# The last pair of down tiles of two feed-forwards: eight of 22 inner tiles by seven block products

## The chip, the cores and the metric

The kernel runs on one core of a Trainium2 chip. The metric is the device time of one execution in microseconds (us). Three runs of the kernel before took 1550.16, 1548.57 and 1549.10 us; the median is 1549.1. Engines are called as in the profile: PE is TensorE, whose weight loads (PEld) run beside its matmuls; DVE is VectorE, ACT is ScalarE, POOL is GpSimd, SP is SyncE, which here only issues transfers.

## What is computed

One inference step of one encoder layer, for 512 new frames of one stream and 64 frames of another. The two are put together as 576 token columns; the model is 1024 wide and the feed-forward 2816. All of it is fp32.

```python
h = LN1(alpha*x + 0.5*FFN1(x))
z = h @ w_in            # mLSTM q,k,v,o,i,f | attention q,k,v | branch gates
h = LN2(alpha*h + w_out(sig(g_m)*P_m(mLSTM(h)) + sig(g_a)*P_a(BandAttn(h))))
y = LN3(alpha*h + 0.5*FFN2(h))

def swiglu_ffn(x, w_gu, w_down):
    gate, up = jnp.split(x @ w_gu, 2, axis=-1)
    return (jax.nn.silu(gate) * up) @ w_down
```

The change touches only `@ w_down`, the down projection, in both feed-forwards. Its product has 1024 output rows (8 tiles of 128, called down tiles here, 0 to 7), 2816 inner rows (22 inner tiles of 128) and 576 columns.

## The kernel before

**Numbers.** Every fp32 operand is split into a high part, rounded to fp32r, and a low part, the rest; one product of two tiles is three matmuls: high x high, high x low, low x high (`mm`, line 133). The high part of a weight is made on ACT (`act`, line 147), the low part by a subtraction on DVE (`tt`, line 150). Activations stand in SBUF as such pairs; weights are split as they arrive.

**Order of the work.** PE follows the order in which the program issues its matmuls. The other engines are ordered at compile time by priority; some steps have a raised priority (`HOT`). A small clock in the program (`Order`) adds up an estimate for each matmul, and `later(dt, fn)` issues a step once that clock has gone on by `dt`; `od.force` issues steps early when their result is needed.

**Weights.** `plan` is the list of all weight chunks in the order of use. `pump` issues for each a load into a `wr` tile (two buffers, on SP's queue, line 266) and its split into `wh` and `wl` (four buffers each). `take` gives a chunk to a product, `done` frees it.

**A feed-forward** (`ffn`) makes 22 inner tiles and then the down tiles, in this order: tiles 0 and 1 together (`joined`); the pairs (2, 3) and (4, 5) by `down_pair`, with `DS = (2, 4)`; tiles 6 and 7 (`LAST[n]` = 6) by plain products. An inner dimension of 22 is cut in three chunks, `DC = ((0, 8), (8, 8), (16, 6))`, as first inner tile and number.

**The block products.** In a pair, inner tiles 8 to 15 don't go by plain products but by a scheme of Strassen's kind. The 2 x 8 weight tiles are seen as 2 x 2 blocks of four tiles, the activations as 2 x 2 blocks of four inner tiles by 288 columns (`HT_` = 576 / 2). `seven` then does seven block products instead of eight. Each is four inner tiles x 3 matmuls of 288 columns, into three PSUM banks X, Y and Z. The combined activations (`Inner`) are made once and used by both pairs. The combined weights are made by `split_ds` from two raw chunks, in four steps: "a" (split of the first), "u" (two sums and their split), "t" (two more sums and their split) and "b" (split of half of the second). After each product `step` says what is to be added where: `Norm.take` adds or subtracts a bank to the running tile `d[j]` or `d[j + 1]` of the layer norm on DVE, at `HOT` priority.

**Tiles 6 and 7 before.** `gemm` passes over token halves: tile 6 and tile 7 for the first half of the columns, then both for the second. `HALVES` is 256 and 320 columns in feed-forward 1, and 320 and 256 in feed-forward 2. Each pass goes over all three chunks, so every chunk of the two tiles is loaded and split twice.

**The layer norm behind it** (`Norm`). `collect` adds the bank of one tile and half to `d[j]` and adds to the running sums `s1`, `s2` (`moments`). When tile 7 of a half is in, `stats` makes mean and variance with small matmuls, `rsqrt` the factor (POOL), `centre` subtracts (tiles 6 and 7 on POOL, the rest on DVE), `spread` brings the factor to all partitions by a matmul, and `apply` scales each tile j. In feed-forward 1 `apply` also makes the high and low parts for the next stage, whose first products (`gemm` with `WAVE_M`, four weight chunks) start with the first half. In feed-forward 2 the first half is scaled and stored to `y` in the same way; the second half is turned to token rows by transposes, scaled and stored (`turned`, output `yt`), which ends the kernel.

**Residuals.** `fetch` loads the residual of a tile into `d[j]`; `residual` scales it and subtracts the shift by halves, `whole` does the same for the whole tile at once.

Of the kernel before, what the change touches and what calls it, by code (L numbers as in the profile page):

```python
# [86 lines left out]
def tile_layer(ctx: ExitStack, tc: tile.TileContext, ins, outs):  # L87
# [30 lines left out]
    def away(s):  # L118

        return dram.tile([P, T], F32, name=nm(s))  # L120
# [88 lines left out]
    def split_ds(c):  # L209

        what = plan[c][0][2]
        hi = wpool.tile([P, 1024], F32R, tag="wh", name=nm("wh"), bufs=NWB)
        lo = wpool.tile([P, 1024], F32R, tag="wl", name=nm("wl"), bufs=NWB)
        if what in ("a", "u"):
            ds[what] = raws.pop(c)
        r1 = ds["a"]

        def put(a, t):
            n = t.shape[1]
            ds["hi"] = act(hi[:, a:a + n], t)  # L220
            tt(lo[:, a:a + n], t, f(hi[:, a:a + n]), ALU.subtract)

        if what == "a":
            put(0, r1)
        elif what == "u":
            own = plan[c][0][0] == "dsap" and plan[c][0][1] > 0
            room = lambda: (slot(F32, opool[0], "o") if own else slot(F32))[:, :512]
            q = ds["q"] = [room() for _ in range(2)]
            ds["r"] = [room() for _ in range(2)] if own else [q[1]] * 2
            r2 = ds["u"]  # L230
            for i in range(2):
                tt(q[i], (r1[:, 512:], r2[:, :512])[i], r2[:, 512:], ALU.add)
            for i in range(2):
                put(512 * i, q[i])
        elif what == "t":
            q = ds.pop("q")[1]
            for i, r in enumerate(ds.pop("r")):
                tt(r, q, r1[:, 512 * (1 - i):512 * (2 - i)], ALU.add)
                q = r
                put(512 * i, r)  # L240
            ds["t"] = ds["hi"]
        else:
            put(0, ds.pop("u")[:, :512])
            del ds["a"]
        parts[c] = (hi, lo)
# [92 lines left out]
    def gemm(tiles, xs, cbs, passes=NORMAL, tags=None):  # L338

        ids = {}  # L340
        pss = {}
        last = {}
        for p, (tl, _) in enumerate(passes):
            for t in tl:
                last[t] = p
        for p, (tl, hl) in enumerate(passes):
            nch = len(tiles[tl[0]])
            k0 = 0
            for c in range(nch):
                for t in tl:  # L350
                    if (t, c) not in ids:
                        ids[t, c] = take(tiles[t][c][0])
                nk = tiles[tl[0]][c][1]
                for i in range(nk):
                    k = k0 + i
                    ww = slice(i * P, (i + 1) * P)
                    st, sp = k == 0, c == nch - 1 and i == nk - 1
                    for t in tl:
                        wh, wl = parts[ids[t, c]]
                        for hf in hl:  # L360
# [12 lines left out]
                k0 += nk  # L373
            for t in tl:
                for hf in hl:
                    cbs[t](hf, pss[t, hf][:, :HALVES[hf][1]])
# [23 lines left out]
                        cbs[t](hf, pss[t, hf])  # L400

    def one(key):
        return [[(key, KT)]]


    w_in = ins["w_in"]
    DC = ((0, 8), (8, 8), (16, 6))

    DS = (2, 4)

    stops = []

    def plan_ffn(n):
        for j in range(CL[n]):
            for e in range(2):
                plan.append(((f"gu{n}", j, e), ins[f"w_gu{n}"][e * FT + j]))
        stops.append(len(plan))
        order = [(j, c) for c in range(3) for j in range(2)]
        for j in DS:
            order += [(j + 1, 0), (j + 1, 2)] + [(j, x) for x in "autb"] + [(j, 0), (j, 2)]  # L420
        order += [(j, c) for j in (*range(LAST[n], KT), *range(LAST[n], KT)) for c in range(3)]
        for j, c in order:
            if c in ("a", "u"):
                plan.append(((f"ds{n}", j, c), ins[f"w_dn{n}"][j + (c == "u")][:, KT * P:2 * KT * P]))
                continue
            if c in ("t", "b"):
                plan.append(((f"ds{n}", j, c), None))
                continue
            k0, nk = DC[c]
            plan.append(((f"dn{n}", j, c), ins[f"w_dn{n}"][j][:, k0 * P:(k0 + nk) * P]))  # L430
# [407 lines left out]
    def seven(name, j, blocks, X, Y, Z, step):  # L838

        ids = {}  # L840

# [10 lines left out]
                       skip_group_check=True)  # L852
                od.tick()

        own = name == "dsap"
        product(X, "a", 1, "b11", True, False)
        step(1)
        product(Y, "a", 0, "b21", True, own)
# [294 lines left out]
            ln.take(j, cc, ps, ALU.add, True)  # L1153


    XD = [away("xd") for _ in range(KT)]

    def ffn(xs, n, gi, raw, final=None, prev=None):
        hh = {}
        with tc.tile_pool(name=nm("hr"), bufs=FT, side="right", reuse_waits="tile") as hr, \  # L1160
# [15 lines left out]
                return cb  # L1176

            def key(j, e):
                return [((f"gu{n}", j, e), KT)]


            combos = Combos(xs, raw, [hr.tile([P, T], F32, tag="h", name=nm("h"), bufs=FT + 1) for _ in range(8)])
# [70 lines left out]
            with tc.tile_pool(name=nm("h1"), bufs=n1, side="right", reuse_waits="tile") as h1, \  # L1253
# [420 lines left out]
    def g59_cb(hf, ps):  # L1674
        act(hs(g59, hf), ps)

    gemm([[(("in", 48), KT)], [(("in", 40), KT)], [(("in", 32), KT)], [("if", KT)]], H,
         [out_cb(vf0, "v", 0), out_cb(kf0, "k", 0), q0_cb, gate_cb], WAVE_M)
    gemm(one(("in", 59)), H, [g59_cb])
    for i in range(4):  # L1680
# [10 lines left out]
    with tc.tile_pool(name="cx", bufs=1, side="right", reuse_waits="tile") as cx:  # L1691
# [511 lines left out]
    gemm([[(("o", j), KT)] for j in (5, 6, 7)], mg, [ln2.cb(j) for j in (5, 6, 7)], SKEW3, ["mm", "mm", "aux"])  # L2203
    rstack.close()
    gate_close()
    ln3 = ffn(ln2.out, 2, 2, ln2.d, outs["y"], ln2)
# [90 lines left out]
```

## Time and profile before

| | us |
|---|---|
| median of three runs | 1549.1 |
| span of the profiled execution, first to last instruction | 1546.8 |
| PE busy | 1531.3 |
| DVE busy | 1160.4 |
| ACT busy | 882.5 |
| POOL busy | 196.6 |
| tiles 6 and 7 of feed-forward 1, on PE | 358.5 to 395.2 |
| tiles 6 and 7 of feed-forward 2, on PE | 1498.0 to 1535.4 |

The page and the views give times from the start of the span. The profiled execution has no time of its own beside the span; the runs' median is 2.3 us longer. A row of a timeline has start, duration, engine, line, operation, the tile written and those read, their shapes, a count if several are merged, and in brackets the time the engine was idle before it and what ended that. A row of a table of stretches has, for each engine, the busy time and the number of instructions, then the granted TensorE clock, the share of the DMA engines and GB/s. Matmul ends are modelled, so gaps and rates are read from starts.

### The profile page before, as it was taken

What the parts mean: (1) busy time and instruction counts of PE and PEld (TensorE: products, weight loads), DVE (VectorE), ACT (ScalarE), POOL (GpSimd) and SP (SyncE); (2) the same over time, 40 slices, a digit from 0 to 9 for tenths busy, and PEclk for the clock granted to TensorE, in tenths of its full rate; (3) what the DMA queues carried; (4) which work ended last, traced back from release to release, by engine and by line L of the source; (5) the groups of instructions that cost most, each with busy time, mean ns of one, the idle gap of its engine ahead of it and who ended that gap; (6) DMA issues with size and microseconds to landing.
All of it is one profiled execution on the core that took longest, in us unless ns stands there. A gap on an engine that the chain in (4) does not pass through costs nothing.

```text
span 1546.8 us, 29458 instructions
## 1 busy us (share of the span) xinstructions
PE 1531.3 (99%) x11587; PEld 1516.3 (98%) x11587; DVE 1160.4 (75%) x2186; ACT 882.5 (57%) x1670; POOL 196.6 (13%) x370
## 2 busy tenths in 40 slices
PE   9999999999999999999999999999999999999997
PEld 9999999999999999999999999999999999999997
DVE  7877778756899767887677577775688787787756
ACT  7545446533766557777864877753456454557323
POOL 1000000100200015545200321102120000001000
PEclk9999999999999999999999999999999999999999
DMA  8322223535544449687544965542653223217244
GB/s 246 109 101 91 93 99 102 130 108 146 172 152 143 156 167 239 153 209 169 139 107 147 283 148 133 130 132 82 199 126 104 108 82 110 82 69 190 78 128 150
DMA packets 82228, 213.18 MB, mean 138 GB/s; under 512 B 9513, under 2 KB 23209, under 8 KB 82089
## 3 DMA queue, kind: packets, MB, share of 16 engines
q1 hardware_dynamic: 66088, 172.29, 33.8%
q0 software_dynamic: 14848, 37.30, 13.7%
q8 instruction: 91, 1.49, 0.4%
q10 hardware_dynamic: 1152, 1.70, 0.3%
q14 instruction: 49, 0.39, 0.1%
HBM read 174.82 MB, written 22.22 MB: 127 GB/s over the span
## 4 chain that ended last, share of the span: by engine, by line
PE 84%; DVE 7%; ACT 3%; DMA 3%; issue 2%; POOL 1%; SPq 0%; ACTq 0%; DVEq 0%; POOLq 0%
PE mm L133 69%; PE aux L133 14%; PE aux L143 2%; DVE wl L150 1%; DVE sc L1537 1%; DVE s L150 1%; DVE s L153 1%; ACT wh L147 1%; ACT sc L147 1%; DMA s<-in_xT 1%; DVE o L150 1%; DVE kl L150 1%; DVE sc L157 1%; DMA wr<-in_w_ap 0%; DMA kh<-kh 0%
## 5 line engine op out<-in xcount | busy, mean ns | idle before, releaser
L133 PE MATMUL mm<-s,wh 128*128 128x288 f32 (+2 forms) x3430 | 700.8, 298 | 0.7 <-DVE s L150 0.2
L133 PEld LDWEIGHTS mm<-s,wh 128*128 128x128 f32 x3430 | 548.3, 189 | 3.8 <-DVE s L150 1.6
L133 PE MATMUL mm<-s,wl 128*128 128x288 f32 (+2 forms) x1705 | 503.3, 295 | 0.0
L133 PEld LDWEIGHTS mm<-s,wl 128*128 128x128 f32 x1705 | 321.1, 188 | 0.2 <-DVE wl L150 0.2
L147 ACT ACTIVATE wh<-wr 128x1024 fp32r<-128x1024 f32 (+2 forms) x136 | 133.0, 979 | 141.0 <-PE mm L133 81.7
L133 PE MATMUL mm<-tx,wh 128*128 128x288 f32 x778 | 158.4, 296 | 0.0
L150 DVE TENSOR_TENSOR wl<-wr,wh 128x1024 fp32r<-128x1024 f32 (+2 forms) x97 | 108.9, 1126 | 57.1 <-ACT wh L147 57.0
L133 PEld LDWEIGHTS mm<-tx,wh 128*128 128x128 f32 x778 | 124.9, 188 | 0.0
L133 PE MATMUL mm<-tx,wl 128*128 128x288 f32 x383 | 113.0, 295 | 0.6 <-DVE wl L150 0.6
L925 ACT ACTIVATE wh<-wt 128x1024 fp32r<-128x1024 f32 x53 | 56.2, 1060 | 88.4 <-DVE wt L150 88.4
L150 DVE TENSOR_TENSOR wl<-wt,wh 128x1024 fp32r<-128x1024 f32 x53 | 64.7, 1222 | 52.3 <-ACT wh L925 51.0
L133 PE MATMUL mm<-h,wh 128*128 128x256 f32 (+2 forms) x384 | 78.3, 295 | 0.0
L150 DVE TENSOR_TENSOR wl<-wu,wh 128x1024 fp32r<-128x1024 f32 x50 | 61.2, 1224 | 21.6 <-ACT wh L925 21.6
L197 POOL DMA_DIRECT2D s<-s x16 | 13.7, 854 | 495.0 <-ACT s L147 252.8
L133 PEld LDWEIGHTS mm<-tx,wl 128*128 128x128 f32 x383 | 72.0, 188 | 0.9 <-DVE wl L150 0.9
L147 ACT ACTIVATE h<-h 128x288 f32<-128x288 f32 x80 | 34.9, 437 | 65.2 <-DVE h L150 65.1
L925 ACT ACTIVATE wh<-wu 128x1024 fp32r<-128x1024 f32 x50 | 52.9, 1058 | 32.7 <-PE mm L133 32.5
L150 DVE TENSOR_TENSOR wl<-ws,wh 128x1024 fp32r<-128x1024 f32 x53 | 64.6, 1219 | 0.1
L150 DVE TENSOR_TENSOR ws<-wu 128x1024 f32<-128x1024 f32 x53 | 64.5, 1217 | 0.0
L133 PEld LDWEIGHTS mm<-h,wh 128*128 128x128 f32 x384 | 61.5, 188 | 0.2
L925 ACT ACTIVATE ah<-wu 128x512 fp32r<-128x512 f32 x53 | 33.4, 631 | 44.8 <-PE mm L133 41.3
L133 PE MATMUL mm<-h,wl 128*128 128x256 f32 (+2 forms) x192 | 56.5, 294 | 0.0
(399 smaller groups left out, 3612.6 us busy)
## 6 DMA issues: line engine op xcount, KB each, us to landing
wu<-in_w_gu SPq DMA_DIRECT2D x80, 512.0 KB, 4.3
wr<-in_w_in SPq DMA_DIRECT2D x46, 512.0 KB, 3.7
wr<-in_w_dn SPq DMA_DIRECT2D x40, 512.0 KB, 3.6
wl<-in_w_in POOLq DMA_DIRECT2D x38, 512.0 KB, 6.8
wu<-in_w_in SPq DMA_DIRECT2D x26, 512.0 KB, 4.5
wr<-in_w_dn SPq DMA_DIRECT2D x20, 384.0 KB, 3.7
s<-s POOLq DMA_DIRECT2D x16, 288.0 KB, 3.7
wr<-in_w_ap SPq DMA_DIRECT2D x8, 512.0 KB, 3.6
```

The lines of the kernel that those rows point to most:

```text
L133: PE.matmul(out, lhsT, rhs, start=start, stop=stop, **kw)
L143: PE.transpose(out, in_, idn)
L147: return ACT.activation(out, in_, func, **kw)
L150: return (eng or DVE).tensor_tensor(out, a, b, op=op)
L153: return DVE.scalar_tensor_tensor(out=out, in0=a, scalar=s, in1=b, op0=op0, op1=op1)
L157: return (eng or DVE).tensor_scalar(out=out, in0=a, scalar1=s1, scalar2=s2, op0=op0, **kw)
L197: return POOL.dma_start(lo, src, accum_op=ALU.add)
L925: self.last = ACT.activation(hi, src, AF.Copy)
L1537: DVE.tensor_tensor_reduce(out=out, in0=ps, in1=g, op0=ALU.add, op1=ALU.min, scale=-1.0, scalar=3e38, accum_out=acc)
```

## The change

A third pair, `DL = 6`, takes inner tiles 8 to 15 by `seven`, in front of the plain passes, in both feed-forwards. The plain passes over halves then go over chunks 0 and 2 only. Since the plain products of the two tiles come after and by halves, all results of the block products are added to `d[6]` and `d[7]` by `Norm.take` (`last_pair`), and Y and Z are closed at the end of `seven` (`own`). The residuals of tiles 6 and 7 are made by `whole`, ahead of `last_pair`, and no longer wait for the last `take` of the pair before. In `split_ds` the two sums of this pair share one room, a free tile of the pool of inner tiles, so that sum and split follow one another by halves. A chunk's key now carries its first inner tile, so that `gemm` can leave one out.

```diff
@@ split_ds @@
+            single = plan[c][0][0] != "dsap" and plan[c][0][1] == DL
+            q = ds["q"] = [ds["room"]()] * 2 if single else [room() for _ in range(2)]
-            q = ds["q"] = [room() for _ in range(2)]
...
-            for i in range(2):
-                tt(q[i], (r1[:, 512:], r2[:, :512])[i], r2[:, 512:], ALU.add)
-            for i in range(2):
-                put(512 * i, q[i])
+            for g in ((0,), (1,)) if single else ((0, 1),):
+                for i in g:
+                    tt(q[i], (r1[:, 512:], r2[:, :512])[i], r2[:, 512:], ALU.add)
+                for i in g:
+                    put(512 * i, q[i])
...
-            ds["t"] = ds["hi"]
+            ds["t", plan[c][0][1]] = ds["hi"]
@@ gemm @@
-                nk = tiles[tl[0]][c][1]
+                k0, nk = tiles[tl[0]][c][1]
...
-                    st, sp = k == 0, c == nch - 1 and i == nk - 1
+                    st, sp = c == i == 0, c == nch - 1 and i == nk - 1
@@ plan_ffn @@
-        order += [(j, c) for j in (*range(LAST[n], KT), *range(LAST[n], KT)) for c in range(3)]
+        order += [(DL, x) for x in "autb"]
+        order += [(j, c) for j in (*range(LAST[n], KT), *range(LAST[n], KT)) for c in (0, 2)]
@@ seven @@
-        own = name == "dsap"
+        own = own or name == "dsap"
@@ new @@
+    def last_pair(n, inner, ln):
+
+        j = DL
+        A, B = slice(0, HT_), slice(HT_, T)
+        X, Y, Z = bank("mm")[:, :HT_], bank("aux")[:, :HT_], bank("mm")[:, :HT_]
+
+        def step(n):
+            if n in (1, 3):
+                ln.take(j, (A, B)[n // 2], X, ALU.add)
+            elif n in (2, 6):
+                ln.take(j, (A, B)[n // 4], Y if n == 2 else Z, ALU.add)
+            elif n in (4, 5, 7):
+                ln.take(j + 1, A if n == 7 else B, Z if n == 4 else X, ALU.subtract)
+
+        seven(f"ds{n}", j, inner.b, X, Y, Z, step, True)
@@ ffn @@
+                ds["room"] = lambda: hr.tile([P, T], F32, tag="h", name=nm("q"), bufs=FT + 1)[:, :512]
...
-                with tc.issue_after(ds["t"].ins):
+                with tc.issue_after(ds["t", DS[-1]].ins):
                     for j in range(LAST[n], KT):
                         ln.fetch(j, ACT)
-                with tc.issue_after(ln.taken.ins):
-                    for j in range(LAST[n], KT):
-                        for hf in range(2):
-                            ln.residual(j, hf)
+                for j in range(LAST[n], KT):
+                    ln.whole(j)
+                last_pair(n, inner, ln)
                 for j, hl in [(j, (hf,)) for hf in (0, 1) for j in range(LAST[n], KT)]:
-                    gemm([[((f"dn{n}", j, c), nk) for c, (_, nk) in enumerate(DC)]], hp_, [ln.cb(j)], (((0,), hl),))
+                    gemm([[((f"dn{n}", j, c), DC[c]) for c in (0, 2)]], hp_, [ln.cb(j)], (((0,), hl),))
```

More of the change, by code (lines that the diff above doesn't have):

```diff
@@ L347, in gemm @@
             nch = len(tiles[tl[0]])
-            k0 = 0
             for c in range(nch):
@@ L372, in gemm @@
                         done(ids[t, c])
-                k0 += nk
             for t in tl:
@@ L402, in one @@
     def one(key):
-        return [[(key, KT)]]
+        return [[(key, (0, KT))]]
     w_in = ins["w_in"]
@@ L409, in tile_layer @@
     DS = (2, 4)
+    DL = 6
     stops = []
@@ L836, in rest, with seven @@
                 self.b[i].update(b11=(h1[:, a], l1[:, a]), b21=(h2[:, a], l2[:, a]), b22=(h2[:, b], l2[:, b]))
-    def seven(name, j, blocks, X, Y, Z, step):
+    def seven(name, j, blocks, X, Y, Z, step, own=False):
         ids = {}
@@ L1178, in key @@
             def key(j, e):
-                return [((f"gu{n}", j, e), KT)]
+                return [((f"gu{n}", j, e), (0, KT))]
             combos = Combos(xs, raw, [hr.tile([P, T], F32, tag="h", name=nm("h"), bufs=FT + 1) for _ in range(8)])
@@ L1675, in g59_cb @@
         act(hs(g59, hf), ps)
-    gemm([[(("in", 48), KT)], [(("in", 40), KT)], [(("in", 32), KT)], [("if", KT)]], H,
+    gemm([[(("in", 48), (0, KT))], [(("in", 40), (0, KT))], [(("in", 32), (0, KT))], [("if", (0, KT))]], H,
          [out_cb(vf0, "v", 0), out_cb(kf0, "k", 0), q0_cb, gate_cb], WAVE_M)
@@ L2202, in tile_layer @@
         gemm(one(("o", j)), mg, [ln2.cb(j)])
-    gemm([[(("o", j), KT)] for j in (5, 6, 7)], mg, [ln2.cb(j) for j in (5, 6, 7)], SKEW3, ["mm", "mm", "aux"])
+    gemm([[(("o", j), (0, KT))] for j in (5, 6, 7)], mg, [ln2.cb(j) for j in (5, 6, 7)], SKEW3, ["mm", "mm", "aux"])
     rstack.close()
```

## The prediction

> **What bounds the kernel now.** I read the page's busy shares first, then the waits of TensorE, then the stretches around the end of each feed-forward, then single instructions there.
>
> ```profile
> PE 1531.3 (99%) x11587; PEld 1516.3 (98%) x11587; DVE 1160.4 (75%) x2186; ACT 882.5 (57%) x1670; POOL 196.6 (13%) x370
> ```
> ```profile
> PE mm L133 <- DVE s L150: 0.2, 1, 0.2
> ```
> ```profile
> core 0: us, PE busy (x) PEld busy (x) DVE busy (x) ACT busy (x) POOL busy (x), PEclk, DMA share, GB/s
> 358.30:374.20 15.90, 15.90 (x136) 15.90 (x136) 10.58 (x18) 6.09 (x8) 0.00 (x0) 1.00 0.44 125
> 374.20:395.20 21.00, 21.00 (x146) 20.90 (x145) 18.10 (x37) 12.47 (x26) 2.75 (x5) 1.00 0.48 145
> ...
> 408.90:435.70 26.80, 26.19 (x185) 25.79 (x185) 24.16 (x46) 22.45 (x46) 2.84 (x5) 1.00 0.52 137
> ```
>
> TensorE is busy 1531.3 of 1546.8 us, so matmul time taken away is time gained, as long as its operands keep up. The rows follow feed-forward 1 from its last two down tiles (358.3 to 395.2) into the next stage. Before 374 VectorE (DVE) has slack: 10.58 of 15.90. From there on it has little: 18.10 of 21.00, then 24.16 of 26.80. That stretch holds the layer norm of the first token half, which must be ready when TensorE starts on w_in at 395.2. Only one wait of 0.2 us shows there, so the two arrive together today.
>
> **TensorE's account.** The first instruction of each half-pass and of the stage behind it, and a run of 288-column products:
>
> ```profile
> 358.52 0.40 PE L133 MATMUL mm<-h,wh 128*128 128x256 f32 x2
> ...
> 374.06 0.45 PE L133 MATMUL mm<-h,wh 128*128 128x320 f32 x2
> ...
> 395.18 0.40 PE L133 MATMUL mm<-s,wh 128*128 128x256 f32 x2
> ...
> 397.69 0.77 PE L133 MATMUL mm<-s,wh 128*128 128x256 f32 x2
> ...
> 1517.42 0.40 PE L133 MATMUL mm<-h,wh 128*128 128x256 f32 x2
> ```
> ```profile
> 1464.89 11.11 PE aux L133 x84
> ```
>
> A half-pass is 2 tiles x 22 inner tiles x 3 = 132 matmuls. 374.06 - 358.52 = 15.54 us gives 0.1177 us for 256 columns. 84 matmuls of 288 columns take 11.11, or 0.1323 each. The difference over 32 columns puts 320 columns at 0.1467, so the second half is 19.36 us of matmuls and some 1.76 us of norm sums. The change drops 8 inner tiles x 3 x 2 tiles = 48 matmuls from each half: 48 x 0.1177 + 48 x 0.1467 = 12.69 us. It adds seven products of 12 matmuls at 288 columns, 84 x 0.1323 = 11.11 us. Net -1.58 us for each feed-forward, -3.16 for both: the gain if every operand is in time.
>
> **Weights.** Per feed-forward four 1024-wide chunks go (load, high part on ACT, low part on DVE); two loads come (quadrants a and u) with one split of 1024, five of 512 and four sums of 512.
>
> ```profile
> L147 ACT ACTIVATE wh<-wr x136: 613/1060/1083, 19.4 to 1525.9; 128x1024 fp32r<-128x1024 f32 x101, 128x768 fp32r<-128x768 f32 x20, 128x512 fp32r<-128x512 f32 x15
> L150 DVE TENSOR_TENSOR wl<-wr,wh x97: 684/1221/1759, 24.1 to 1527.9; 128x1024 fp32r<-128x1024 f32 x63, 128x768 fp32r<-128x768 f32 x20, 128x512 fp32r<-128x512 f32 x14
> ```
> ```profile
> wr<-in_w_dn SPq DMA_DIRECT2D x8, 512.0 KB, 3.5
> ```
> ```profile
> 350.00 1.06 ACT L147 ACTIVATE wh<-wr 128x1024 fp32r<-128x1024 f32 x1 [0.96 <-DMA wr<-in_w_dn]
> ```
>
> With the medians for 1024 columns and the minima for 512, ACT: -4 x 1.06 + 1.06 + 5 x 0.61 = about 0; DVE: -4 x 1.22 + 1.22 + 9 x 0.68 = +2.5 us. That lies under the plain and block products up to 369, where DVE is busy no more than 10.58 of 15.90 us. I cost it at nothing; without that slack it is 2.5. Quadrant u's data arrive where the second chunk of tile 6 arrives now, at 350.0. Its two halves share one room, so sum, high, low, sum, high, low run one after the other: 4 x 0.68 + 2 x 0.61 = 3.9, done at 354, wanted at 363.3 (358.5 + 3 x 1.59). t needs as long again from 353.7, when the plain products leave their first chunk (358.5 - 36 x 0.1323): 357.6, wanted at 361.7. Both have 4 us and more. The raw a and u are held in the only two load buffers until t and b are made (about 357 and 361), and the loads queued behind them on SP wait. At 3.5 + 1.06 + 1.22 = 5.8 us a load and two buffers, a chunk comes every 2.9 us. Half-pass chunks are eaten at 24 x 0.1177 = 2.8 and 18 x 0.1177 = 2.1, from 369.6 on. Reckoned from 357 and 361, each split waiting also for a part that the block products free, the chunks are ready at 364, 368, 370, 374 and wanted at 369.6, 372.4, 374.5, 377.3: the cover is 3 us at its thinnest. Nothing; a late chunk would cost up to 2.9 us.
>
> **Norm 1, first half: the cover shrinks.** Its rows on DVE, and one of ACT:
>
> ```profile
> 374.26 0.42 DVE L150 TENSOR_TENSOR s<-mm,s 128x256 f32<-128x256 f32 x1 [0.16 <-PE mm L133]
> ...
> 375.96 0.42 DVE L150 TENSOR_TENSOR s<-s,sq 128x256 f32<-128x256 f32 x1 [0.81 <-ACT sq L147]
> ...
> 378.75 0.97 DVE L150 TENSOR_TENSOR dg<-ident,rs 128x256 f32<-128x256 f32 x1 [0.61 <-POOL rs L533]
> 379.65 1.76 DVE L150 TENSOR_TENSOR wl<-wr,wh 128x1024 fp32r<-128x1024 f32 x1
> ...
> 385.49 0.96 DVE L150 TENSOR_TENSOR wl<-wr,wh 128x768 fp32r<-128x768 f32 x1 [1.21 <-ACT wh L147]
> ...
> 397.60 0.83 DVE L150 TENSOR_TENSOR s<-s,s 128x256 fp32r<-128x256 f32 x2 [1.73 <-ACT s L147]
> ```
> ```profile
> 395.70 0.63 ACT L147 ACTIVATE wh<-wr 128x512 fp32r<-128x512 f32 x1 [1.75 <-DMA wr<-in_w_in]
> ```
> ```profile
> 378.71 1.62 POOL L150 TENSOR_TENSOR s<-s,c 128x256 f32<-128x256 f32 x2
> ```
>
> The seven additions and subtractions that the block products send out of PSUM are like the one at 374.26, 0.42 us for 256 columns; another product of 1.59 us runs before their bank is written again, so they cost nothing (without that, 7 x 0.42 = 2.9).
>
> The norm's chain runs from the last sum of the half (374.26) to the last low part (398.43): 24.2 us, under which lies the second half-pass. TensorE's 397.69 pair of matmuls takes 0.77 instead of 0.40: it waited 0.37 for that last part. With the change the first half ends at 358.5 + 11.11 + 84 x 0.1177 = 379.5, 5.4 us later than now, and TensorE comes to w_in at 395.18 - 1.58 = 393.6. The chain must be 7.0 us shorter to cost nothing. What can shorten it: two chunks fewer to split (1.22 + 0.96 = 2.2), and idle time of 0.81 + 0.61 + 1.21 + 1.73 = 4.4, of which 2.9 goes back to late weights (the 1.73 to ACT waiting for a load at 395.70, which starts earlier when the chunks are fewer). All of it makes 6.6, none of the idle 2.2. I take the 2.2, the 2.9 and half the other 1.4: 5.8 of the 7.0. The last part then comes at 398.4 + 5.4 - 5.8 = 398.0, against 398.43 now, and as the sums for the second half stand behind that matmul in TensorE's order, the stage follows: -0.4 instead of -1.58. Bounds: -1.95 (1.58 and the 0.37), and 5.4 - 2.2 = +3.2 when no idle time is won back.
>
> By the Trainium skill, page SBUF — State Buffer, section "SBUF: two separate sides", a GpSimd operation and a VectorE one with two SBUF inputs lock each other out of a shared port for a whole instruction. The trace agrees in kind: the 1024-wide subtraction at 379.65, beside POOL's, took 1.76 instead of 1.22. By that rule a DVE with no gap left would lose POOL's whole 1.62 and not 0.54, and feed-forward 1 would come to +0.7.
>
> **Norm 3 and the end.** In feed-forward 2 the first half has 320 columns and the second 256.
>
> ```profile
> 1530.63 2.84 DVE L153 SCALAR_TENSOR_TENSOR s<-s,cols,aux 128x320 f32<-128x320 f32 x6
> 1535.58 0.42 DVE L150 TENSOR_TENSOR s<-mm,s 128x256 f32<-128x256 f32 x1 [2.11 <-PE mm L133]
> 1537.53 0.16 DVE L153 SCALAR_TENSOR_TENSOR var<-aux,m 128x2 f32<-128x2 f32 x1 [1.52 <-ACT m L147]
> ...
> 1540.40 2.73 DVE L153 SCALAR_TENSOR_TENSOR s<-s,rs,s 128x512 f32<-128x512 f32 x4
> ```
> ```profile
> 1529.88 5.97 SPq L762 DMA_DIRECT2D out_y<-s  x8
> 1541.17 2.32 SPq L720 DMA_DIRECT2D out_yt<-s  x4
> ```
>
> The eight scale steps of the first half now end 2.11 us before the last sum at 1535.58. They move: first half over at 1517.4 + 4.0 = 1521.4 (11.11 + 84 x 0.1467 for 19.4), last sum at 1534.0. By the code's own clock some four of the eight are issued only behind the final half's work. They need 4 x 0.47 = 1.9 us of DVE, and 2.11 + 1.52 us are idle around the last sum. I let them fit: -1.58. Without that cover they stand behind the 1540.40 group, and four y stores (2.32 for four) follow the last store: -1.58 + 2.32 = +0.7.
>
> **Sum.** -0.4 - 1.58 = -2.0. Against the profiled 1546.8 this is 1544.8; the runs' median, 1549.1, lies 2.3 above that span, so 1547.1.
>
> **Rivals.** (1) *Both covers hold*: the idle time goes entirely, TensorE's account stands, and the 0.37 goes too: -3.5, 1545.6. For it: the 2.9 us of idle caused by weight loads. Against it: DVE's 18.10 of 21.00. (2) *Norm of the first half uncovered*: VectorE can't win its idle time back, as each piece hangs on another engine. It decides as soon as less than 3.8 us of the 7.0 is found in norm 1: feed-forward 1 then loses over 1.6, as much as feed-forward 2 gains. Price +3.2 there and, as the same chain is late at norm 3, up to +0.7: +3.9, 1553.0. For it: the stage behind, busy 24.16 of 26.80, cannot absorb anything. Against it: 2.9 us of idle have a cause that goes. The Trainium skill, TensorE: Matmul & The Clock Gate, Part 1, says a window of about 3.4 us without matmuls halves the clock; 3.2 us stays under it, and every stretch above was granted 1.00, so no run shows it here. (3) *Only the stores are late*: norm 1 as forecast, norm 3 at +0.7: +0.3, 1549.4.
>
> **How the numbers follow.** Chances: forecast 0.39, rival 1 0.29, rival 2 0.22, rival 3 0.10. The range reaches from rival 1 (less 0.4 for scatter) almost to rival 2: 1545.2 to 1552.6; the forecast's own is 1546.0 to 1549.0. A measurement can tell about 0.2%, 3.1 us, from no change: faster means under 1546.0, slower over 1552.2. Faster: rival 1 (0.27) and a little of the forecast (0.05), 0.32. Slower: 0.19 of rival 2 and 0.04 of the rest, 0.23. Same: 0.45.
>
> **What would show it.** Right: 84 matmuls of 288 columns in 11.1 us without a wait in them; the half-passes at about 9.9 and 14.1 us; the last low part of norm 1's first half near 398.0, with TensorE waiting some 2 us there. Rival 1: no wait, last low part by 396. Rival 2: it comes after 399.5, and the whole of w_in shifts. Rival 3: y stores behind the last store of the final half. Wrong altogether: a wait of TensorE for weights inside the block products or the half-passes.

## The result, and the profile after

| | before | after |
|---|---|---|
| median of five runs, us | 1548.57 | 1558.11 |
| lowest and highest, us | 1548.09 to 1550.16 | 1556.24 to 1562.84 |
| span of the profiled execution, us | 1546.8 | 1559.8 |

The ratio after to before is 1.0063, with a 95% interval from 1.0050 to 1.0077: about 9.8 us longer. That is outside the range forecast, on the slow side. The profiled execution of the changed kernel is the longest of its five (1562.84); the spans of the other four lie between 1554.5 and 1557.4. So places in its trace are read below as differences between two instructions near each other, not as the whole span.

From the page of the changed kernel, the busy times and the granted clock in 40 slices:

```profile
PE 1538.5 (99%) x11563; PEld 1519.8 (97%) x11563; DVE 1170.7 (75%) x2208; ACT 882.4 (57%) x1674; POOL 197.0 (13%) x370
...
PEclk9999999999799999999999999999999999999999
```

TensorE has 24 instructions fewer than before, and is busy 7.2 us longer. The clock has one dent, in the eleventh slice of 39 us, which is 390 to 429 us: the beginning of the stage behind feed-forward 1. Before it was at full speed there. The waits of TensorE in the changed kernel:

```profile
PE mm L133 <- DVE s L150: 3.1, 8, 0.9
...
PE mm L133 <- ACT s L147: 1.5, 2, 1.3
...
PE mm L133 <- ACT wh L147: 1.1, 1, 1.1
```

The kernel before has one wait for DVE's `s`, of 0.2 us; it is at 309.17, in the pair (2, 3), and not at w_in, where the prediction took it to be. Of the eight in the changed kernel, two are at w_in (398.65 and 401.19), one is at 340.94 (below), four are in the pairs (2, 3) and one is in a later stage. Both waits for ACT's `s` are at w_in (395.90 and 403.27); the one for `wh` is in feed-forward 2 (below). None is longer than 1.3 us. Rows that merge several matmuls hide waits inside them, so what w_in loses is read from starts. The stretches at the end of feed-forward 1 and behind it, in the changed kernel (columns as in the table of stretches in the prediction; the granted clock is the third number from the end):

```profile
389.00:396.00 7.00, 6.79 (x47) 6.53 (x45) 7.00 (x17) 4.34 (x10) 1.18 (x3) 1.00 0.40 128
396.00:403.30 7.30, 4.94 (x16) 3.09 (x16) 5.70 (x15) 7.27 (x17) 2.33 (x5) 0.67 0.86 309
403.30:410.00 6.70, 6.70 (x27) 6.13 (x28) 1.20 (x3) 1.14 (x4) 0.01 (x1) 0.50 0.80 212
410.00:417.00 7.00, 7.00 (x37) 6.84 (x37) 4.04 (x8) 0.46 (x2) 2.91 (x3) 0.60 0.00 0
```

Two things go wrong one after the other. From 396 to 403.3 TensorE gets through 16 matmuls, which are 16 x 0.1177 = 1.9 us of work, while DVE and then ACT (7.27 of 7.30) are full. From 403.3 on it is "busy" all the time, but at half the clock. How much each costs is read from single instructions, first of the changed kernel and then of the kernel before:

```profile
381.09 0.45 PE L133 MATMUL mm<-h,wh 128*128 128x320 f32 x2
...
395.16 0.41 PE L133 MATMUL mm<-s,wh 128*128 128x256 f32 x2
...
403.27 1.04 PE L133 MATMUL mm<-s,wh 128*128 128x256 f32 x2 [1.28 <-ACT s L147]
...
404.96 0.63 PE L133 MATMUL mm<-s,wh 128*128 128x256 f32 x2
...
420.28 0.46 PE L133 MATMUL mm<-s,wh 128*128 128x320 f32 x2
```
```profile
398.42 0.40 PE L133 MATMUL mm<-s,wh 128*128 128x256 f32 x2
...
409.25 0.45 PE L133 MATMUL mm<-s,wh 128*128 128x320 f32 x2
```

The first instruction on `s` (395.16 after, 395.18 before) starts w_in. Its first tile needs a new part of the norm for each of its eight inner tiles; the ninth group of matmuls (404.96 after, 398.42 before) is the first that needs nothing new, and the first with 320 columns starts the other half of the tokens. From the start to the ninth group: 9.80 after, 3.24 before, so **6.6 us of waits**. From there to the other half: 15.32 after, 10.83 before, so **4.5 us of half clock**. Together 11.1. The clock falls already at 398.50 (last section), so a part of the 6.6 is half clock too. The second half-pass ahead of it (381.09 to 395.16) took 14.07 us, as forecast.

At the end of the kernel, on SP's queue in the changed kernel, the `y` stores stand ahead of the `yt` stores, and nothing is late behind them:

```profile
1547.68 4.34 SPq L764 DMA_DIRECT2D out_y<-s  x8
1554.42 2.32 SPq L722 DMA_DIRECT2D out_yt<-s  x4
```

One more wait is new, in each feed-forward, where the third pair begins to prepare. DVE and then PE in the changed kernel:

```profile
338.41 0.76 DVE L153 SCALAR_TENSOR_TENSOR s<-s,c 128x576 f32<-128x576 f32 x1 [2.88 <-DMA s<-in_xT]
...
339.69 0.75 DVE L153 SCALAR_TENSOR_TENSOR s<-s,c 128x576 f32<-128x576 f32 x1
340.35 0.44 DVE L150 TENSOR_TENSOR s<-s,mm 128x288 f32<-128x288 f32 x1
```
```profile
339.77 0.29 PE L133 MATMUL aux<-h,wl 128*128 128x288 f32 x1
340.94 0.37 PE L133 MATMUL mm<-s,wh 128*128 128x288 f32 x1 [0.88 <-DVE s L150]
```

The first row is `whole`, the residual of tile 6. It stands at the head of DVE's queue and waits 2.88 us for its load. A weight split, the residual of tile 7 and the `take` of the pair before (340.35) stand behind it, and TensorE waits for the bank that this `take` empties: it starts at 340.94 instead of 339.77 + 0.13, so 1.0 us late. Feed-forward 2 has the same picture (3.09 us, and 1.1 us of TensorE, at 1493.57). There the profile names a weight's high part on ACT, which ended at 1493.44; the `take` ended at 1493.42, and in both feed-forwards TensorE starts 0.15 us behind its end.

### The profile page after: what moved, and what is told of

Its sections match the earlier page's. It is cut to its first block, busy times and chain, and to the rows that moved or that the text cites. A ratio compares the mean times of both kernels' runs of the same rounds, so it can differ in the third digit from the quotient of the medians.

```text
span 1559.8 us, 29436 instructions
## 1 busy us (share of the span) xinstructions
PE 1538.5 (99%) x11563; PEld 1519.8 (97%) x11563; DVE 1170.7 (75%) x2208; ACT 882.4 (57%) x1674; POOL 197.0 (13%) x370
## 4 chain that ended last, share of the span: by engine, by line
PE 75%; DVE 10%; ACT 6%; issue 4%; DMA 4%; POOL 1%; DVEq 0%; SPq 0%; ACTq 0%; POOLq 0%
PE mm L133 62%; PE aux L133 12%; DVE wl L150 2%; PE aux L143 1%; ACT wh L147 1%; ACT s L147 1%; DVE s L150 1%; DMA wr<-in_w_dn 1%; DVE sc L1555 1%; DMA s<-s 1%; DVE s L153 1%; DVE sc L157 1%; DVE U L153 1%; DVE o L150 1%; ACT sc L147 1%
## 5 line engine op out<-in xcount | busy, mean ns | idle before, releaser
L133 PE MATMUL mm<-s,wh 128*128 128x288 f32 (+2 forms) x3494 | 720.5, 299 | 6.1 <-DVE s L150 3.0
L133 PEld LDWEIGHTS mm<-s,wh 128*128 128x128 f32 x3494 | 562.8, 190 | 12.0 <-DVE s L150 3.6
L133 PE MATMUL mm<-s,wl 128*128 128x288 f32 (+2 forms) x1737 | 514.7, 296 | 0.0
L133 PEld LDWEIGHTS mm<-s,wl 128*128 128x128 f32 x1737 | 329.5, 190 | 0.0
L147 ACT ACTIVATE wh<-wr 128x1024 fp32r<-128x1024 f32 (+2 forms) x132 | 127.8, 970 | 132.9 <-PE mm L133 74.7
L150 DVE TENSOR_TENSOR wl<-wr,wh 128x768 fp32r<-128x768 f32 (+2 forms) x93 | 102.3, 1103 | 43.5 <-ACT wh L147 43.4
L133 PE MATMUL mm<-h,wh 128*128 128x288 f32 (+2 forms) x324 | 66.1, 294 | 0.0
L133 PE MATMUL aux<-h,wh 128*128 128x288 f32 (+2 forms) x276 | 56.4, 294 | 0.0
L927 ACT ACTIVATE wh<-ws 128x1024 fp32r<-128x1024 f32 x53 | 55.8, 1053 | 0.7 <-PE mm L133 0.4
```

The source lines that it names most:

```text
L133: PE.matmul(out, lhsT, rhs, start=start, stop=stop, **kw)
L147: return ACT.activation(out, in_, func, **kw)
L150: return (eng or DVE).tensor_tensor(out, a, b, op=op)
L927: self.last = ACT.activation(hi, src, AF.Copy)
```

## The experiments

The kernel before ran beside each, and every ratio is to it, with its 95% interval. In all variants of the changed kernel the rest is as in the changed kernel.

**Which feed-forward loses.** The third pair in one feed-forward only; the other keeps its plain passes over three chunks and its residuals behind the last `take`.

```diff
+    PAIR = (1,)          # and (2,)
-        order += [(DL, x) for x in "autb"]
+        order += [(DL, x) for x in "autb"] if n in PAIR else []
...
-        order += [(j, c) ... for c in (0, 2)]
+        order += [(j, c) ... for c in ((0, 2) if n in PAIR else (0, 1, 2))]
```

Feed-forward 1 only:

> The third pair in feed-forward 1 alone; feed-forward 2 as before. Theory A (the loss lies at the norm behind feed-forward 1, where TensorE waits for the first half and its clock then drops): +9 to +10.5 us against the kernel before, nearly all of what the whole change costs. Theory B (the block products of the third pair or their weights cost in both feed-forwards alike): about +5 us.

Feed-forward 2 only:

> The third pair in feed-forward 2 alone. Theory A: -0.3 us against the kernel before, from -1.6 of matmuls, +1.1 of the wait for quadrant b at the start of the pair before and +0.2 at the end; within -1 to +0.5. Theory B: about +5 us.

Measured: 1.0058 (1.0043 to 1.0073), some 9.0 us, for feed-forward 1 alone; 0.9998 (0.9989 to 1.0008) for feed-forward 2 alone. The loss is all in feed-forward 1. Feed-forward 2 doesn't lose, but doesn't gain its 1.58 us either.

**Waits and clock apart.** While the first tile of w_in waits, TensorE is given work that nobody reads: four matmuls of 256 columns on constant weights, into a bank of their own, ahead of each of seven inner tiles, 28 in all.

```diff
                 for i in range(nk):
+                    if idles and p == 0 and i:
+                        for _ in range(4):
+                            PE.matmul(idles[0], ones_r, hs(xs.get(0, 0)[0], 0), start=True, stop=True)
```

> As the changed kernel, but ahead of each inner tile but the first of the first w_in tile TensorE runs four more matmuls of 256 columns on data that are there, into a bank that nobody reads (28 in all, 28 x 0.1177 = 3.3 us if they ran alone). Theory A (the half clock that follows the waits costs 4 to 5 us): the clock stays at 1.00 from 396 to 415 and the time is 1553 to 1554, +4.5 to +5.5 against the kernel before. Rival (the late norm alone sets the stage behind it, and the clock costs nothing beside it): 1558 to 1561.

Measured: 1.0048 (1.0033 to 1.0062), 7.4 us longer than before, against 9.8 without the fill. The stretches of this kernel, and two of its instructions:

```profile
396.00:403.30 7.30, 6.43 (x41) 5.16 (x42) 6.17 (x16) 7.30 (x17) 1.26 (x3) 1.00 0.89 301
403.30:410.00 6.70, 6.63 (x53) 6.24 (x52) 2.73 (x6) 1.53 (x5) 3.35 (x4) 1.00 0.83 224
```
```profile
404.30 0.40 PE L133 MATMUL mm<-s,wh 128*128 128x256 f32 x2
...
414.83 0.46 PE L133 MATMUL mm<-s,wh 128*128 128x320 f32 x2
```

The clock is 1.00 throughout. The last low part of the norm ends at 403.91, against 404.01 without the fill, and the ninth group comes 9.59 us behind the first one (394.71), against 9.80: the norm is as late as before, and the fill, 28 x 0.1177 = 3.3 us, takes the place of waits. From the ninth group to the other half it takes 10.53 us instead of 15.32. In the trace the clock is worth 4.8 us there. In the medians it is worth 2.4, less than was expected, and the intervals of the two kernels overlap. What follows that point differs by some us between executions, so I tried the same once more on the version with the shortest waits (below), with and without the fill.

**The cover alone.** Is it the block products, or just that less work stands in front of w_in? The kernel before, with one edit: in feed-forward 1 the second half-pass of tiles 6 and 7 leaves out inner tiles 8 to 15 (48 matmuls of 320 columns, 7.0 us), and no block product is added. Its `d[6]` and `d[7]` miss that part.

```diff
-        order += [(j, c) for j in (*range(LAST[n], KT), *range(LAST[n], KT)) for c in range(3)]
+        order += [(j, c) for hf in (0, 1) for j in range(LAST[n], KT)
+                  for c in ((0, 2) if n == 1 and hf else (0, 1, 2))]
```

> The kernel before, with no third pair at all, but in feed-forward 1 the second half-pass of tiles 6 and 7 leaves out inner tiles 8 to 15: 48 matmuls of 320 columns, 7.0 us of TensorE work between the end of the first half and w_in, are gone, and the first half ends when it did. Theory A (the norm of the first half needs that cover): the matmuls' 7.0 us come back as waits at w_in, and the clock drops there; time between -1 and +5 us against the kernel before, I expect +2. Rival (the block products or their weights make the loss, not the shorter cover): -5 to -7 us.

Measured: 1.0025 (1.0015 to 1.0035). **7.0 us of matmuls less, and the kernel is 3.9 us longer.** Its instructions and stretches:

```profile
374.03 0.45 PE L133 MATMUL mm<-h,wh 128*128 128x320 f32 x2
...
388.10 0.40 PE L133 MATMUL mm<-s,wh 128*128 128x256 f32 x2
...
399.21 1.27 PE L133 MATMUL aux<-onec,s 128*128 128x1 f32 x6
...
413.35 0.46 PE L133 MATMUL mm<-s,wh 128*128 128x320 f32 x2
```
```profile
388.00:395.00 7.00, 5.63 (x20) 3.56 (x18) 6.63 (x17) 6.97 (x16) 2.40 (x6) 0.76 0.87 275
395.00:402.00 7.00, 5.76 (x23) 5.20 (x24) 0.76 (x2) 2.08 (x7) 0.91 (x1) 0.50 0.99 280
```

TensorE comes to w_in 7.1 us earlier (388.10), and reaches the norm sums of the other half at 399.21; in the kernel before they stand at 399.13. So nearly all of the 7.0 us went into waits. The last low part ends at 396.98, only 1.45 us earlier than in the kernel before (398.43), and the matmuls behind it run at half clock: the norm sets this point. Then the clock is at 0.50, and the other half starts at 413.35 instead of 409.25, 4.1 us late. The same kernel with eight fill matmuls ahead of each of the seven inner tiles:

> As the run that left out 48 matmuls of cover, with eight extra matmuls of 256 columns ahead of each inner tile but the first of the first w_in tile (56, or 6.6 us if they ran alone, in waits of about 8 us). The computation leaves out the same products as that run. Theory A: the clock stays at 1.00, the waits still give back the 7.0 us, and the time is that of the kernel before within 1 us, against +3.9 without the extra matmuls. Rival (the 3.9 us came from the norm's own lateness and not from the clock): +3 to +5 again.

Measured: 1.0008 (0.9999 to 1.0017), 1.2 us. Its stretch at the same place has the full clock:

```profile
395.00:402.00 7.00, 7.00 (x59) 6.84 (x58) 1.89 (x7) 2.55 (x6) 2.04 (x3) 1.00 0.83 248
```

The fill is 56 x 0.1177 = 6.6 us and takes the place of nearly all waits, so this run doesn't show how long TensorE would have waited at the full clock. But the last low part ends at 397.01, as without the fill (396.98): the norm doesn't get faster, and at most 1.4 of the 7.0 us could be gained. The other half starts at 408.14, 1.1 us before its place in the kernel before and 5.2 us earlier than without the fill. So the waits eat most of the 7.0 us of saved work, and what makes the kernel longer than the one before is the clock, 2.7 us by the medians; the 1.2 us that are left can't be told from nothing.

**What sets the norm's end: pace or load.** In `apply` the program's own clock issues the eight scale steps 860 ns apart. Issued 450 ns apart in norm 1's first half:

```diff
-            later(860 * j, lambda j=j: self.apply(j, hf, rb))
+            later((450 if self.gi == 0 and hf == 0 else 860) * j, lambda j=j: self.apply(j, hf, rb))
```

> As the changed kernel, but the eight scale steps of norm 1's first half are issued 450 ns of the program's clock apart instead of 860, so all of them are issued ahead of the next stage's first weights. Theory C (the last two scale steps stand behind 2.1 us of the next stage's weights on ScalarE because they are issued later): the last low part comes 2 us earlier and the time falls by 2 to 4 us, to +5.5 to +7.5 against the kernel before. Rival (VectorE's and ScalarE's load sets the chain, whatever the order): within 1 us of the changed kernel, +8.5 to +10.5.

Measured: 1.0063 (1.0048 to 1.0078), no gain. The last low part starts at 402.43, about 1 us earlier than in the changed kernel. From the first sum (380.88) to its end the chain takes 21.96 us, against 22.72, so the pace is worth 0.8 us of it; the clock falls all the same:

```profile
402.43 0.41 DVE L150 TENSOR_TENSOR s<-s,s 128x256 fp32r<-128x256 f32 x1
```

The other explanation is DVE's own load. The first three w_in tiles use the high part of their weights where the low part belongs, which takes six subtractions of 512 columns off DVE (what those products compute is not the full product):

```diff
-                    lo = wpool.tile([P, 1024], F32R, tag="wl", name=nm("wl"), bufs=NWB)
+                    lo = hi if plan[c][0] in PIECES else wpool.tile([P, 1024], F32R, tag="wl", name=nm("wl"), bufs=NWB)
...
+                        if plan[c][0] in PIECES:
+                            continue
```

> As the changed kernel, but the first three w_in tiles use their high part in place of their low part, so that VectorE has six subtractions of 512 columns (6 x 0.60 = 3.6 us) less in the norm's stretch; TensorE and ScalarE do the same work as before. Theory D (VectorE's load stretches the norm's chain): the last low part comes 2 to 3.6 us earlier, about 401, and the time falls by 2 to 5 us, to +4.5 to +7.5 against the kernel before. Rival (ScalarE's load and the dependencies set the chain): the last low part within 1 us of 404, the time unchanged, +8.5 to +10.5.

Measured: 1.0029 (1.0020 to 1.0038), 4.5 us instead of 9.8. First and last step of the chain on DVE in this kernel, then in the changed one:

```profile
381.67 0.42 DVE L150 TENSOR_TENSOR s<-mm,s 128x256 f32<-128x256 f32 x1 [0.67 <-PE mm L133]
...
399.66 0.76 DVE L150 TENSOR_TENSOR s<-s,s 128x256 fp32r<-128x256 f32 x2 [0.15 <-ACT s L147]
```
```profile
381.29 0.42 DVE L150 TENSOR_TENSOR s<-mm,s 128x256 f32<-128x256 f32 x1 [0.91 <-PE mm L133]
...
403.25 0.76 DVE L150 TENSOR_TENSOR s<-s,s 128x256 fp32r<-128x256 f32 x2 [1.32 <-ACT s L147]
```

From the first sum to the end of the last low part the chain takes 18.75 us instead of 22.72: 4.0 less, where six subtractions at 0.60 from start to start come to 3.6. DVE's load sets the chain. The fall of the time, 5.3 us, isn't from the chain alone: the half clock lasted 3.4 us here instead of 17.1 (last section). ACT's load was not varied by itself.

**The residuals.** `whole` behind the last `take` of the pair before, as the halves were in the kernel before:

```diff
-                for j in range(LAST[n], KT):
-                    ln.whole(j)
+                with tc.issue_after(ln.taken.ins):
+                    for j in range(LAST[n], KT):
+                        ln.whole(j)
```

> As the changed kernel, but the two whole-tile residual steps wait for the last take of the pair before, as the half-tile ones did. Theory A (a residual step at the head of VectorE's queue waits about 3 us for its transfer and keeps quadrant b of the pair before from being split in time, about 1 us of TensorE in each feed-forward): -2 us against the changed kernel, +7.5 against the one before. Rival (that wait of TensorE is there for another reason): no change, +9.5.

Measured: 1.0077 (1.0062 to 1.0092), not better but, if anything, worse. DVE and then PE in this kernel:

```profile
362.35 1.42 DVE L153 SCALAR_TENSOR_TENSOR s<-s,c 128x576 f32<-128x576 f32 x2
363.69 0.45 DVE L150 TENSOR_TENSOR s<-s,mm 128x288 f32<-128x288 f32 x1
```
```profile
364.28 0.50 PE L133 MATMUL mm<-s,wh 128*128 128x288 f32 x2 [1.26 <-DVE s L150]
```

The expectation named the split of quadrant b; by the rows it is the bank that TensorE waits for. The wait at 340 is gone, but the residuals now run directly ahead of the first `take` of the third pair itself, and TensorE waits 1.26 us for that bank. Both places are wrong. In between, after the block products of the pair (4, 5) and before its plain products end, nobody waits for DVE; there the residuals are put with a mark of its own, `ln.mid`, in the kernel with the pair in feed-forward 2 alone:

```diff
         seven(f"ds{n}", j, inner.b, X, Y, Z, step)
+        ln.mid = ln.taken
...
+                    with tc.issue_after(ln.mid.ins):
+                        for j in range(LAST[n], KT):
+                            ln.whole(j)
```

> The third pair in feed-forward 2 alone, its two whole-tile residual steps bound behind the last take of the block products of the pair before, which puts them beside that pair's plain products. Theory A: the wait of about 1.1 us that the third pair alone left in feed-forward 2 goes, and no other takes its place: -1.4 us against the kernel before, -0.6 to -1.9. Rival (another wait takes its place, as the 1.3 us one did when these steps were put behind the last take): 0.

Measured: 0.9991 (0.9982 to 1.0000), 1.4 us shorter than before. The trace shows no wait of TensorE in feed-forward 2, and the residuals run without one:

```profile
1488.10 0.75 DVE L153 SCALAR_TENSOR_TENSOR s<-s,c 128x576 f32<-128x576 f32 x1
...
1490.11 0.75 DVE L153 SCALAR_TENSOR_TENSOR s<-s,c 128x576 f32<-128x576 f32 x1
```

This is the one version here that is not longer than the kernel before, so it was run a second time on another chip:

> The version with the third pair in feed-forward 2 alone and its residual steps beside the plain products of the pair before, timed once more, since its first interval reached from -2.8 us to 0. If the gain of about 1.4 us is real, the ratio comes out between 0.9985 and 0.9996 again; if it was chance, at 1.0000 or above.

Measured: 0.9991 (0.9982 to 1.0000) again, 1548.20 against 1550.06. Two intervals that end at 1.0000 make a gain of some 1.4 us likely; it stays below the 0.2% that one measurement can tell. The traces tell it more sharply. From the last `aux` matmul of the pair (4, 5) to the norm's sums behind the second half-pass TensorE takes 37.85 us in the kernel before (1497.53 to 1535.38), 36.27 in the first of these two runs (1497.61 to 1533.88) and 36.28 in the second (1499.85 to 1536.13): 1.58 and 1.57 less.

**All remedies together**, in both feed-forwards: residuals at `ln.mid`, 450 ns, and the 28 fill matmuls.

> The whole change with three mends: the residual steps beside the plain products of the pair before, the scale steps 450 ns apart, and the 28 extra matmuls that keep TensorE's clock up at w_in. Theory A with C: 9.5 - 2 (residual steps) - 2 (scale steps) - 2 to 4 (clock) = +1.5 to +3.5 us against the kernel before: what is left is the shorter cover. Rival (something else costs as much): +5 or more.

Measured: 1.0015 (1.0006 to 1.0024), 2.3 us. And without the fill:

> As the run with three mends, without the 28 extra matmuls: the clock alone is told apart. Theory A: the clock falls to half for some 8 us from about 398 on, and the time is 2 to 4.4 us longer than with them, +4.3 to +6.7 against the kernel before. Rival (the extra matmuls did nothing, the two other mends made the whole difference): +2.3, as with them.

Measured: 1.0048 (1.0035 to 1.0060), 7.4 us. These two intervals don't overlap: 0.0033 x 1549 = 5.1 us for the clock by the medians. In the two traces it is 3.3: from the start of w_in to the other half TensorE takes 19.27 us with the fill (393.77 to 413.04) and 22.53 without (394.25 to 416.78). But also with everything mended, feed-forward 1 has not been brought to gain from the third pair. The kernel before takes 14.07 us for that stretch (395.18 to 409.25), so 5.2 us are lost there, of which the fill itself may be a part. Less 1.58 in each feed-forward this makes 2.0, near the 2.3 measured.

## Why the prediction was wrong, step by step

**TensorE's account: right.** Second half-pass 14.07 us (forecast 14.1), block products with the first half 21.2 (forecast 21.0), no wait inside either. From the last `aux` matmul of the pair (4, 5) to the start of w_in feed-forward 1 takes 35.61 us (359.55 to 395.16) instead of 37.19 (357.99 to 395.18): 1.58 less, to the digit. So does feed-forward 2 with the residuals well placed (1.58 and 1.57).

**Weights: right.** No wait for a weight inside the third pair or the half-passes; the 0.4 us for `wl` that is left in the stage behind (420 to 450 us) was 0.6 before.

**Norm 3 and the stores: right.** The `y` stores stay ahead of `yt`. With the residuals well placed the time from the sums to the end is 11.55 us, against 11.41 before, so the 1.58 us arrive at the end almost whole.

**Norm 1, first half: the step that failed.** It said that the chain would find 5.8 of the 7.0 us that it has to be shorter. It found 1.5: 381.29 to 404.01 is 22.7 us, against 24.2. That is past the point of rival 2 (less than 3.8 found), which was given 0.22. (That the norm and TensorE arrived together in the kernel before rests on 397.69 alone, as the 0.2 us wait lies elsewhere.) The chain as one stretch, before and then after; the third pair of numbers is DVE's busy time and count:

```profile
374.26:398.43 24.17, 24.10 (x169) 23.79 (x168) 19.60 (x41) 15.20 (x32) 4.78 (x10) 1.00 0.52 153
```
```profile
381.29:404.01 22.72, 20.15 (x116) 17.82 (x115) 19.71 (x43) 15.21 (x32) 5.89 (x11) 0.88 0.62 209
```

Two terms of the sum failed. The 2.2 us of splits that go gave nothing, as DVE is busy 19.60 us in the chain before and 19.71 after. And of its idle time, 4.57 before and 3.01 after, 1.6 us were won, where 3.6 were counted (the 2.9, and half of the other 1.4). Where the first went is shown by DVE's low parts of weights within the chain, before and then after:

```profile
L150 DVE TENSOR_TENSOR wl<-wr,wh x8: 684/822/1759, 376.3 to 394.0; 128x512 fp32r<-128x512 f32 x4, 128x768 fp32r<-128x768 f32 x2, 128x1024 fp32r<-128x1024 f32 x2
```
```profile
L150 DVE TENSOR_TENSOR wl<-wr,wh x8: 676/678/1220, 383.3 to 399.5; 128x512 fp32r<-128x512 f32 x6, 128x1024 fp32r<-128x1024 f32 x1, 128x768 fp32r<-128x768 f32 x1
```

Eight splits in both. Two chunks are gone, as the prediction counted (2.2 us). But the next stage's weights are prepared at the same times as before, while the chain ends 5.6 us later. So two of w_in's pieces (398.51 and 399.45, before 398.34 and 399.34; 2 x 0.68) and the low part of its gate chunk, which goes to a `wh` tile (400.13, before 400.00; 0.67), lie inside the chain now. With one addition of squares for the second half (0.48) 2.5 us come back. Of the 4.4 us of idle in the chain's rows, 3.0 remain (0.75, 0.61, 0.28 and 1.32). The 2.9 us that were to go back to late weights were two pieces: the 1.21 went, and the 1.73 ahead of the last low parts is still there as 0.28 and 1.32. With the weights in time DVE is full (7.00 of 7.00 from 389 to 396), and ACT, which makes the high parts and a part of the scaling, is the next engine to be late (7.27 of 7.30). The run with six subtractions fewer shows DVE's load as the cause; the run with closer steps shows that pace is worth less than 1 us.

The rule on the shared port from the Trainium skill, SBUF — State Buffer, section "SBUF: two separate sides", which the prediction weighed, explains no difference, as what DVE loses is the same before and after. POOL's two subtractions in the changed kernel, five of DVE beside them, and four of DVE alone in the kernel before:

```profile
386.42 1.61 POOL L150 TENSOR_TENSOR s<-s,c 128x256 f32<-128x256 f32 x2
```
```profile
387.36 2.30 DVE L150 TENSOR_TENSOR s<-s,c 128x256 f32<-128x256 f32 x5
```
```profile
381.33 1.42 DVE L150 TENSOR_TENSOR s<-s,c 128x256 f32<-128x256 f32 x4
```

The four alone took 1.42 from first start to last end. With 0.42 for one that is 0.33 from start to start, and five come to 1.75. So 0.55 us is lost, as much as before (1.76 - 1.22). Whether POOL's whole 1.61 is lost can't be read: the product `dg` ahead of these rows, also beside POOL, took 0.97 in both kernels (378.75 and 386.46), and no trace has it without POOL beside it. If it took 0.42 alone, as others of 256 columns do, another 0.55 is lost there, 1.1 in all.

**The price of rival 2: the mechanism was named, but half of the price was missing.** It had the late norm at +3.2 for feed-forward 1 against the kernel before, and nothing for the clock. The last low part came 5.6 us late by TensorE's own time (404.01 - 395.16 = 8.85, against 398.43 - 395.18 = 3.25), and the remaining matmuls of the tile made 6.6 of it, as they already ran at half clock. Then 4.5 us of half clock follow. The prediction set the clock aside with the Trainium skill, TensorE: Matmul & The Clock Gate, Part 1, saying that a wait of 3.2 us stays under its window of 3.4 us without matmuls. The trace doesn't agree with that reading: between 394 and the fall at 398.50 the longest wait listed for TensorE is 0.2 us, none later is longer than 1.3, and the clock falls. What counted here was how little was done over a stretch, some ten matmuls in the 3.41 us ahead of the fall, and not one long gap; with the fill in the waits it didn't fall.

**What was not in the sum at all: the residuals.** The change takes away the condition on which they were issued, and the prediction has no term for it. The residual step of tile 6, issued earlier than its data, stood at the head of DVE's queue for 2.88 and 3.09 us. That cost 1.0 and 1.1 us of TensorE, which is why feed-forward 2 alone came out at 0.9998.

Put together, from the traces: feed-forward 1 has -1.58, + 1.0 for the residuals, + 6.6 waits, + 4.5 clock, which is 10.5; feed-forward 2 has -1.58 + 1.1, which is -0.5. The sum of 10.0 stands against 9.8 measured by the medians. The two profiled executions differ by 13.0; the other 3 us lie mostly in the pairs (2, 3) (0.7 and 1.2) and between 815 and 935 us (1.5). In these places the traces of other variants are also later than that of the kernel before, by up to 0.7, 1.0 and 1.9 us (0.7 also where feed-forward 1 is as before), so they are not put down to the change.

## What to carry to other kernels

Matmul time at the end of a stage may be the cover for the vector work that the next stage waits for: before taking it away, measure the chain of that work, count what its engine has to do in that time including the next stage's work that falls into it when it ends later, and expect a full engine to give back nothing. When TensorE comes to wait in small pieces, price the half clock beside the waits; here it was 3 to 5 us by the traces, on top of some 6 us of waits, and a few matmuls that nobody reads removed it. And where a change drops the condition on which an instruction was issued, look up when its data arrive and what stands behind it.

## What the hardware showed that was not expected

**The clock falls and returns in steps.** Narrow stretches around the fall and the return, in the changed kernel:

```profile
398.25:398.50 0.25, 0.20 (x1) 0.01 (x1) 0.25 (x2) 0.25 (x2) 0.00 (x0) 1.00 0.89 361
398.50:398.75 0.25, 0.10 (x1) 0.10 (x1) 0.25 (x2) 0.25 (x2) 0.00 (x0) 0.50 1.23 508
415.25:415.50 0.25, 0.25 (x3) 0.25 (x3) 0.00 (x0) 0.00 (x0) 0.00 (x0) 0.50 0.00 0
415.50:415.75 0.25, 0.25 (x4) 0.25 (x4) 0.00 (x0) 0.00 (x0) 0.00 (x0) 0.87 0.00 0
```

the kernel with all remedies but the fill:

```profile
400.00:400.25 0.25, 0.20 (x1) 0.19 (x1) 0.22 (x1) 0.25 (x1) 0.00 (x0) 0.93 1.00 410
...
410.25:410.50 0.25, 0.25 (x3) 0.25 (x3) 0.25 (x2) 0.00 (x0) 0.25 (x1) 0.59 0.00 0
```

and the kernel without six low parts:

```profile
399.75:400.00 0.25, 0.25 (x1) 0.11 (x1) 0.25 (x1) 0.18 (x1) 0.00 (x0) 0.67 0.90 360
...
403.25:403.50 0.25, 0.25 (x4) 0.25 (x4) 0.00 (x0) 0.00 (x0) 0.00 (x0) 1.00 1.04 410
```

A stretch whose clock is between 0.50 and 1.00 holds the change; its share tells where. The half clock lasted from 398.50 to 415.56, 17.1 us; from 400.22 to 410.46, 10.2; and from 399.83 to 403.25, 3.4. These are five, three and one times 3.41. The Trainium skill, TensorE: Matmul & The Clock Gate, Part 1, gives the activity window as 3413 ns and free-running, and these lengths agree with it. They also show that one window of work was not always enough to return. In the changed kernel the 3.41 us ahead of the fall hold some ten matmuls, 1.2 us of work. Why it then took five windows in one kernel and one in another isn't settled. The norm's sums, many matmuls of a single column, lie in the windows that didn't bring it back; that they count for little is only my guess.

**What falls cost varies between executions.** The mean granted clock of the five executions of the changed kernel goes from 0.993 (1562.84 us) to 0.996 (1556.24 us). One source is on record. In five of the variants' traces (all remedies with and without the fill, six low parts fewer, the cover with the fill, and the second run of the pair in feed-forward 2 alone) the clock falls once more, for one 3.41 us, somewhere between 630 and 643 us, in a stage that none of the edits touches; the traces of the kernel before and of the changed kernel have no such fall. 3.41 us at half clock hold 1.7 us of work less. It may be a part of why the first fill gained 4.8 us in the trace and only 2.4 in the medians; that, and whether the cost depends on where in a window the waits begin, has not been tested.
